# Converting and splitting each unit of weights in one operation, with three tiles in place of four, in a two-layer encoder

## The chip, the cores and the metric

The kernel runs on one core of one Trainium2 chip. Its time is the device time of one execution in microseconds (us). Before the change the median of three runs is 2588.59 us (2588.29 to 2591.06). A separate execution was profiled; all views of the profile are of that one.

The engines are called PE (matrix products; PEld is its loading of stationary operands), DVE (vector), ACT (scalar), POOL, and SP, whose queue issues the transfers between HBM and on-chip memory (SBUF).

## The reference, cut to what matters

Two layers over 256 tokens of width 2048. All weights are float32 and each is read once.

```python
for l in range(DEPTH):                                  # 2
    mod = c_act @ ada_w[l] + ada_b[l]                   # adaLN: six vectors of 2048
    sh_a, sc_a, gt_a, sh_m, sc_m, gt_m = split(mod, 6)
    h = rmsnorm(x, norm_mix[l]) * (1.0 + sc_a) + sh_a
    qa, ka, va, qb, kb, vb, ga, gb = split_cols(h @ w_in[l])
    ya = window_attention(qa, ka, va, sink_a[l]) @ w_proj_a[l]      # mask |i - j| <= 128
    yb = neighbourhood_attention(qb, kb, vb, rel_bias_b[l]) @ w_proj_b[l]
    x = x + gt_a * ((sigmoid(ga) * ya + sigmoid(gb) * yb) @ w_out[l])
    h = rmsnorm(x, norm_ffn[l]) * (1.0 + sc_m) + sh_m
    u = depthwise_conv(h @ w_up[l], conv_w[l], conv_b[l])
    g, v = split(u, 2)
    x = x + gt_m * ((silu(g) * v) @ w_down[l])
```

## The kernel before

**Products in high and low parts.** PE multiplies operands rounded to a shorter float32 form. To keep float32 accuracy, each operand is split into a high part (the rounded value) and a low part (the rest), and a product is the sum of high x high, high x low and low x high. An ACT copy makes the high part of the weights (line 348), a DVE subtraction the low part (line 349).

**Units of weights.** The host lays out all weight matrices as one sequence of blocks of 128 x 128 in the order of use (`block_stream`, line 100). Sixteen blocks are a unit: 1 MiB, one transfer into a raw tile of 128 x 2048 (line 337). There are 464 units, 232 a layer. `unit_steps` (line 331) takes a raw tile out of four, issues the transfer, and then makes the high and the low part of one half of the unit and of the other, each half in its own `hl` tile of 128 x 2 x 1024, of which there are also four (two units). The raw tile comes free when the second subtraction is done, an `hl` tile when PE has used its eight blocks. `next_block` (line 419) hands out blocks; when a unit is used up it takes the next one, in program order just before that unit's matmuls (in the first 52 units of layer 0 one unit earlier).

**What uses a block.** `feature_block` (line 387) holds the weights still and moves the activations; with `Wide` activations (the FFN) a block is two matmuls, lines 391 and 392, of 512 and 256 columns, so a unit is 32 matmuls; otherwise it is three, lines 395 to 397. `tokens` (line 454, the q, k and v columns) moves the weights instead, lines 464 to 466.

**adaLN.** `ada` (line 229) reads the 12288 x 2048 matrix of a layer as 96 tiles of 1 MiB, and one DVE operation for each (line 248) multiplies it by the activated `c` and sums it up. Except for three tiles at the start these use the same four raw tiles as the weights. `plan` (line 794) sets when they are issued: at the end of a unit, along a table of corners by unit number. In layer 0, between units 108 and 231 that is 63 products, so nearly every second unit. In that stretch (and in layer 1 before unit 76 and from unit 108 on) a product is "patient": its transfer is issued at the end of a unit, and its DVE operation is put in program order behind the splits of the next unit (`use_landed`, line 426) and pinned there.

**Order on the queues.** A framework schedules the program: it gives out tiles as they come free, in the order of the program by priority, and fixes the order of each engine's instructions. SP's queue works in order, so a transfer that waits for a tile holds up those behind it.

**Attention.** Eight heads of mixer A, then eight of mixer B, run as steps between the units. Each head has a score tile `p` out of two. In line 730 DVE adds a mask (A) or a bias (B) to the scores. The mask is one tile that is loaded once (`small`, line 870); the bias of a head is brought by its own transfer into `p` (line 964), one step ahead of its use. In layer 1 all heads, in place of PE, use DVE and POOL to turn the probabilities (`turned_blocks`, line 750).

**Layout.** Several tiles have a few extra columns, and their contents begin 16, 48 or 64 columns in (`OFF`, `ROW`, `led`, `chunks_of`, `paired`); `skip` allocates two small unused tiles.

Of the kernel before, what the change touches and what calls it, by code (L numbers as in the profile page):

```python
# [9 lines left out]
F32 = mybir.dt.float32  # L10
# [126 lines left out]
OFF, ROW = 48, 64  # L137
SPARE = {"y2": ROW}
# [7 lines left out]
def encoder(ctx: ExitStack, tc: tile.TileContext, a: dict, out: bass.AP):  # L146
    nc = tc.nc
    pool = lambda name, bufs, **kw: ctx.enter_context(tc.tile_pool(name=name, bufs=bufs, **kw))
    skips = []

    def skip(n, p=None):

        skips.append((p or pool(f"skip{len(skips)}", 1)).tile([P, n // 4], F32, name=f"skip{len(skips)}"))
        nc.vector.memset(skips[-1][:], 0.0)

    const = pool("const", 1)
    lay = pool("lay", 2)
    rawp = pool("raw", 4)
    hlp = pool("hl", 4)
# [30 lines left out]
    skip(96, const)  # L190
    skip(224)
# [5 lines left out]
    def chunks_of(p, tag, room, name, n=None, apart=True):  # L197

        n = n or room
        t = p.tile([P, room * 2 * S + SPARE.get(tag, 0)], F32R, name=name, tag=tag)
        at = [2 * S * k + (ROW - OFF if apart and k == n - 1 and (k < room - 1 or tag in SPARE) else 0) for k in range(n)]
        return [t[:, i : i + 2 * S].rearrange("p (a s) -> p a s", a=2) for i in at]

    def led(name, apart=None):

        t = hp.tile([P, KC * 2 * S + OFF + ROW], F32R, name=name, tag="h")
        at = [0] + [OFF + 2 * S * k for k in range(1, KC)]
        if apart:  # L210
            at[apart] += ROW - OFF
            at[apart + 1 :] = [i + ROW for i in at[apart + 1 :]]
        return [t[:, i : i + 2 * S].rearrange("p (a s) -> p a s", a=2) for i in at]

    def paired(dt, name, at=ROW - OFF):

        t = ev.tile([P, 2 * S + ROW], dt, name=name, tag="u", bufs=2)
        return t[:, at : at + 2 * S].rearrange("p (a s) -> p a s", a=2)
# [112 lines left out]
    def unit_steps(l, u, by_halves=False):  # L331

        raw = rawp.tile([P, UB * P], F32, name=f"w{l}_{u}", tag="raw")
        if not by_halves:
            nc.sync.dma_start(raw[:], a["ws"][l, u])
        halves = []
        streamed = any(m == "w_in" and mo < GATE_A // P for m, _, mo in STREAMS[l][u * UB : (u + 1) * UB])
        at = OFF if streamed else 0  # L340
        for j in range(2):
            n = UB * P // 2
            hl = hlp.tile([P, 2 * n + ROW], F32R, name=f"hl{l}_{u}_{j}", tag="hl")
            hl = hl[:, at : at + 2 * n].rearrange("p (a n) -> p a n", a=2)
            r = raw[:, j * n : (j + 1) * n]
            if by_halves:
                nc.sync.dma_start(r, a["ws"][l, u][:, j * n : (j + 1) * n])
            nc.scalar.copy(hl[:, 0], r)  # L348
            nc.vector.tensor_tensor(out=hl[:, 1], in0=r, in1=hl[:, 0].bitcast(F32), op=ALU.subtract)  # L349
            halves.append(hl)  # L350
            if j == 0:
                yield halves
# [34 lines left out]
    def feature_block(ps, hl, j, act, first, last):  # L387

        hi, lo = hl[:, 0, j * P : (j + 1) * P], hl[:, 1, j * P : (j + 1) * P]
# [9 lines left out]
    class Stream:  # L399
# [54 lines left out]
        def tokens(self, h, kcs):  # L454

            pss = [mm.tile([P, 512], F32, name=f"ps{self.l}_{self.u}_t{t}", tag="mm") for t in range(2)]
            for kc in kcs:
# [3 lines left out]
                hi, lo = (turns(hl[:, i, j * P : (j + 4) * P]) for i in range(2))  # L461
# [44 lines left out]
    class Squares:  # L506
# [6 lines left out]
        def add(self, mo):  # L513
            sq = self.acc if mo == 0 else ev.tile([P, S], F32, name="sq", tag="r", bufs=2)
# [67 lines left out]
    class Bare:  # L582
# [4 lines left out]
        def __init__(self, l, w, sums):  # L587
# [7 lines left out]
            for tag in homes + ["qn"]:  # L595
# [3 lines left out]
                for i in range(k):  # L599

                    off = 2 * self.half * i + (0 if self.chunks else ROW - OFF)
                    c = t[:, off : off + 2 * self.half].rearrange("p (a s) -> p a s", a=2)
                    self.chunks.append((turns(c[:, 0, : S + 2]), turns(c[:, 1, :S])))
# [21 lines left out]
        def roots(self):  # L625
            self.rbs = spread(self.rs)
            self.h = led(f"h{self.l}_{self.w}")
# [668 lines left out]
```

## Time and profile before

| | us |
|---|---|
| median of three runs | 2588.59 |
| the profiled execution | 2583.21 |
| its span, first to last instruction | 2581.4 |
| PE busy | 2549.9 |
| DVE busy | 2209.4 |
| ACT busy | 1450.7 |
| all splits, line 349, 928 of 1225 ns | 1131.3 |
| all high parts, line 348, 928 of 1046 ns | 965.2 |
| all adaLN products, line 248, 189 of 2350 ns and three more | 443.9 |

The granted clock is 0.999 of full speed. In a list of groups a row is: line, engine, operation, out<-in, shapes, number, then busy time, mean ns of one, idle time ahead and what ended it. In a timeline a row is: start, length, engine and line, operation. Where neighbours overlap, the chain of waits gives the time that each holds it, less than its length. "DMA share" in the table by stretches is the mean busy share of the 16 DMA engines.

### The profile page before, as it was taken

How to read it: one execution, taken by the hardware profiler on the slowest of the kernel's cores; microseconds unless marked ns; L12 is line 12 of the kernel's file. 1: busy time of each engine (PE TensorE's matmuls, PEld its weight loads, DVE VectorE, ACT ScalarE, POOL GpSimd, SP SyncE). 2: the span in 40 equal slices, each digit the busy share in tenths (PEclk: the TensorE clock that was granted, in tenths of full speed). 3: DMA queues.
4: the chain of work that ended last, by engine and by line, in shares of the span. 5: the costliest groups of instructions: out<-in, count | busy, mean ns of one | idle time of the engine just before them, and what ended most of it. 6: DMA issues, size and time to landing. Idle time of an engine off the chain costs nothing.

```text
span 2581.4 us, 43559 instructions
## 1 busy us (share of the span) xinstructions
PE 2549.9 (99%) x17324; PEld 2377.2 (92%) x17324; DVE 2209.4 (86%) x3227; ACT 1450.7 (56%) x2432; POOL 246.0 (10%) x345
## 2 busy tenths in 40 slices
PE   8999999999999999999999999999999999999999
PEld 7999899999999998998898889999999999999998
DVE  8998998998998989889997778878889987766775
ACT  5445765456663655455565666555576546644663
POOL 0001100000000000000002668630000000000000
PEclk9999999999999999999999999999999999999999
DMA  9998789986788777877776657667848775555554
GB/s 369 353 349 306 264 296 353 342 317 224 262 319 304 291 291 293 326 291 282 283 257 246 260 212 256 250 260 291 298 166 293 291 295 198 205 201 198 204 202 147
DMA packets 102158, 699.99 MB, mean 271 GB/s; under 512 B 12865, under 2 KB 15169, under 8 KB 18113
## 3 DMA queue, kind: packets, MB, share of 16 engines
q1 hardware_dynamic: 101954, 697.20, 73.3%
q8 instruction: 136, 2.23, 0.3%
q14 instruction: 68, 0.56, 0.1%
HBM read 695.06 MB, written 2.10 MB: 270 GB/s over the span
## 4 chain that ended last, share of the span: by engine, by line
PE 67%; DVE 19%; ACT 5%; issue 4%; POOL 3%; DMA 3%; ACTq 0%; DVEq 0%; POOLq 0%; SPq 0%
PE ps L391 24%; PE ps L392 12%; DVE hl L349 8%; PE ps L397 7%; PE ps L395 7%; PE ps L396 7%; DVE aw L248 3%; ACT hl L348 3%; PE ps_t L466 2%; PE ps_t L465 2%; PE ps_t L464 2%; DVE u L1135 1%; DMA w<-in_ws 1%; POOL packA L320 1%; POOL p L320 1%
## 5 line engine op out<-in xcount | busy, mean ns | idle before, releaser
L349 DVE TENSOR_TENSOR hl<-w,hl 128x1024 fp32r<-128x1024 f32 x928 | 1131.3, 1225 | 237.9 <-ACT hl L348 235.4
L348 ACT CAST hl<-w 128x1024 fp32r<-128x1024 f32 x928 | 965.2, 1046 | 583.9 <-PE ps L392 231.6
L391 PE MATMUL ps<-h,hl 128*128 128x512 f32 x2432 | 797.4, 382 | 0.0
L392 PE MATMUL ps<-h,hl 128*128 128x256 f32 x2432 | 664.0, 273 | 2.8 <-DVE hl L349 2.8
L391 PEld LDWEIGHTS ps<-h,hl 128*128 128x128 f32 x2432 | 459.7, 189 | 63.7
L392 PEld LDWEIGHTS ps<-h,hl 128*128 128x128 f32 x2432 | 466.9, 192 | 5.7 <-DVE hl L349 5.6
L248 DVE CUSTOM_DVE_ANT_0 aw<-aw,cact,ab 128x2048 f32<-128x2048 f32 x189 | 443.9, 2350 | 11.4 <-DMA aw<-in_aw 11.1
L395 PE MATMUL ps<-h,hl 128*128 128x256 f32 x896 | 247.3, 276 | 1.9 <-DVE ri L745 0.8
L396 PE MATMUL ps<-h,hl 128*128 128x256 f32 x896 | 246.4, 275 | 0.0
L397 PE MATMUL ps<-h,hl 128*128 128x256 f32 x896 | 245.8, 275 | 0.0
L464 PE MATMUL ps_t<-hl,h 128*128 128x512 f32 x576 | 217.6, 382 | 3.5 <-ACT h L571 2.3
L465 PE MATMUL ps_t<-hl,h 128*128 128x512 f32 x576 | 219.2, 381 | 1.4 <-DVE hl L349 1.2
L466 PE MATMUL ps_t<-hl,h 128*128 128x512 f32 x576 | 218.5, 380 | 0.0
L395 PEld LDWEIGHTS ps<-h,hl 128*128 128x128 f32 x896 | 171.9, 192 | 3.1 <-ACT hl L348 1.0
L396 PEld LDWEIGHTS ps<-h,hl 128*128 128x128 f32 x896 | 172.0, 192 | 0.4 <-DVE h L572 0.2
L391 PE MATMUL ps<-act_o,hl 128*128 128x512 f32 x512 | 171.1, 382 | 0.6 <-ACT hl L348 0.6
L397 PEld LDWEIGHTS ps<-h,hl 128*128 128x128 f32 x896 | 171.6, 192 | 0.0
L1135 DVE SCALAR_TENSOR_TENSOR u<-both,cw,u 128x255 f32<-128x255 f32 x304 | 146.0, 480 | 2.9
L392 PE MATMUL ps<-act_o,hl 128*128 128x256 f32 x512 | 139.9, 273 | 1.6 <-DVE hl L349 1.6
L397 PE MATMUL ps<-merged,hl 128*128 128x256 f32 x512 | 140.9, 275 | 0.6 <-DVE hl L349 0.6
L396 PE MATMUL ps<-merged,hl 128*128 128x256 f32 x512 | 140.7, 275 | 0.0
L395 PE MATMUL ps<-merged,hl 128*128 128x256 f32 x512 | 140.5, 275 | 0.0
(242 smaller groups left out, 4852.7 us busy)
## 6 DMA issues: line engine op xcount, KB each, us to landing
w<-in_ws SPq DMA_DIRECT2D x463, 1024.0 KB, 4.8
aw<-in_aw SPq DMA_DIRECT2D x189, 1024.0 KB, 5.2
p<-in_bias SPq DMA_DIRECT2D x16, 256.0 KB, 4.6
x<-in_xT SPq DMA_DIRECT2D x4, 512.0 KB, 5.4
aw_o<-in_aw SPq DMA_DIRECT2D x2, 1024.0 KB, 12.6
out<-x SPq DMA_DIRECT2D x16, 128.0 KB, 2.3
w<-in_ws SPq DMA_DIRECT2D x2, 512.0 KB, 11.8
aw_b<-in_aw SPq DMA_DIRECT2D x1, 1024.0 KB, 18.0
```

What stands on the lines that cost most here:

```text
L248: product = nc.vector.tensor_tensor_reduce(out=raw[:], in0=raw[:], in1=cact[:], scale=1.0, scalar=ab[:, i : i + 1], op0=ALU.mult, op1=ALU. ...
L348: nc.scalar.copy(hl[:, 0], r)
L349: nc.vector.tensor_tensor(out=hl[:, 1], in0=r, in1=hl[:, 0].bitcast(F32), op=ALU.subtract)
L391: nc.tensor.matmul(ps[:], hi, act.both, start=first, stop=False)
L392: nc.tensor.matmul(ps[:, :S], lo, act.high, start=False, stop=last)
L395: nc.tensor.matmul(out, hi, act[0], start=first, stop=False)
L396: nc.tensor.matmul(ps[:, :S], hi, act[1], start=False, stop=False)
L397: nc.tensor.matmul(out, lo, act[0], start=False, stop=last)
L464: nc.tensor.matmul(ps[:], xh, hi, start=kc == kcs[0], stop=False)
L465: nc.tensor.matmul(ps[:], xh, lo, start=False, stop=False)
L466: nc.tensor.matmul(ps[:], xl, hi, start=False, stop=kc == kcs[-1])
L1135: nc.vector.scalar_tensor_tensor(out=u[:, to], in0=ps[:, of], scalar=w[:, j : j + 1], in1=u[:, to], op0=ALU.mult, op1=ALU.add)
```

## The change

It replaces the two half-unit operations by one for the whole unit on ACT and one on DVE (the first unit of all, whose transfer comes in two halves, is still done by halves). A split unit is now one tile of 128 x 2 x 2048, and there are three of them; of raw tiles there are three too. The constants of the adaLN plan stay.

Room is found elsewhere: all extra columns and shifted offsets go, and the `skip` tiles with them; the mask of mixer A is no longer kept but brought from HBM into `p` for every head, directly ahead of that head's scores; the convolution weights `cw` are loaded after the attention into a tile shared with it; the squares `sq` use the tiles of tag `z` instead of two of their own.

```diff
-    rawp = pool("raw", 4)
-    hlp = pool("hl", 4)
+    rawp = pool("raw", 3)
+    hlp = pool("hl", 3)
...
-    skip(96, const)
-    skip(224)
...
-    def led(name, apart=None):
-
-        t = hp.tile([P, KC * 2 * S + OFF + ROW], F32R, name=name, tag="h")
-        at = [0] + [OFF + 2 * S * k for k in range(1, KC)]
...
+    def chunks_of(p, tag, room, name, n):
+
+        t = p.tile([P, room, 2, S], F32R, name=name, tag=tag)
+        return [t[:, i] for i in range(n)]
+
+    def halved(name):
+
+        return chunks_of(hp, "h", KC, name, KC)
...
         raw = rawp.tile([P, UB * P], F32, name=f"w{l}_{u}", tag="raw")
+        hl = hlp.tile([P, 2, UB * P], F32R, name=f"hl{l}_{u}", tag="hl")
+        n = UB * P // 2
+        pieces = [slice(0, n), slice(n, 2 * n)]
+        halves = [(hl[:, 0, r], hl[:, 1, r]) for r in pieces]
         if not by_halves:
+            pieces = [slice(0, 2 * n)]
             nc.sync.dma_start(raw[:], a["ws"][l, u])
-        halves = []
-        streamed = any(m == "w_in" and mo < GATE_A // P for m, _, mo in STREAMS[l][u * UB : (u + 1) * UB])
-        at = OFF if streamed else 0
-        for j in range(2):
-            n = UB * P // 2
-            hl = hlp.tile([P, 2 * n + ROW], F32R, name=f"hl{l}_{u}_{j}", tag="hl")
-            hl = hl[:, at : at + 2 * n].rearrange("p (a n) -> p a n", a=2)
-            r = raw[:, j * n : (j + 1) * n]
+        for r in pieces:
             if by_halves:
-                nc.sync.dma_start(r, a["ws"][l, u][:, j * n : (j + 1) * n])
-            nc.scalar.copy(hl[:, 0], r)
-            nc.vector.tensor_tensor(out=hl[:, 1], in0=r, in1=hl[:, 0].bitcast(F32), op=ALU.subtract)
-            halves.append(hl)
-            if j == 0:
-                yield halves
+                nc.sync.dma_start(raw[:, r], a["ws"][l, u][:, r])
+            nc.scalar.copy(hl[:, 0, r], raw[:, r])
+            nc.vector.tensor_tensor(out=hl[:, 1, r], in0=raw[:, r], in1=hl[:, 0, r].bitcast(F32), op=ALU.subtract)
+            yield halves
...
-            sq = self.acc if mo == 0 else ev.tile([P, S], F32, name="sq", tag="r", bufs=2)
+            sq = self.acc if mo == 0 else ev.tile([P, S], F32, name="sq", tag="z")
...
     def small(l):
 
-        if l == 0:
-            tables.append(load(a["maskA"], [P, 2, S], "maskA"))
...
-        cw = load(a["cw"][l], [P, 2 * FC, 4], f"cw{l}", lay, tag="cw", bufs=1)
...
             p = at.tile([P, 2, S], F32, name="p", tag="p")
+            nc.sync.dma_start(p[:], a["maskA"])
...
             yield from attend(
-                q, k, v, p, tables[0], SCALE, sink[:, i : i + 1], lambda: oA[i], rows if i < MOVED[l][0] else None
+                q, k, v, p, p, SCALE, sink[:, i : i + 1], lambda: oA[i], rows if i < MOVED[l][0] else None
             )
...
         bg.finish(job)
-        merged = led(f"merged{l}")
+        cw = load(a["cw"][l], [P, 2 * FC, 4], f"cw{l}", at, tag="qh", bufs=1)
+        merged = halved(f"merged{l}")
```

More of the change, by code (lines that the diff above doesn't have):

```diff
@@ L195, in place, with paired @@
         return sp.tile([P, n, S], dt, name=name, tag=tag)
[L197 to L204, printed above, removed]
-    def led(name, apart=None):
-        t = hp.tile([P, KC * 2 * S + OFF + ROW], F32R, name=name, tag="h")
-        at = [0] + [OFF + 2 * S * k for k in range(1, KC)]
[L210 to L218, printed above, removed]
+    def chunks_of(p, tag, room, name, n):
[3 more added lines that the diff above has]
+        return chunks_of(hp, "h", KC, name, KC)
+    def paired(dt, name):
+        return ev.tile([P, 2, S], dt, name=name, tag="u", bufs=2)[:]
     mods, amods, nrms, done = {}, {}, {}, {0: 0, 1: 0}
@@ L460, in tokens @@
                 j -= 3
-                hi, lo = (turns(hl[:, i, j * P : (j + 4) * P]) for i in range(2))
+                hi, lo = (turns(half[:, j * P : (j + 4) * P]) for half in hl)
                 for t, ps in enumerate(pss):
@@ L888, in small @@
             rots.append(rot)
-        return gains, sink, cw, rots
+        return gains, sink, rots
     for l in range(L):
@@ L895, in encoder @@
         if l == 0:
[L896 removed]
+            h = halved("h0_0")
             first.append(ada_and_h(first_h(h)))
```

23 lines of the change are left out of this document (7 added, 16 removed).

## The prediction

> **What bounds the kernel now.** I read first the page's head, then a table by stretches (busy time and number of instructions of PE, PEld, DVE, ACT, POOL; then clock, DMA share, GB/s), then who waits for whom.
>
> ```profile
> span 2581.4 us, 43559 instructions
> PE 2549.9 (99%) x17324; PEld 2377.2 (92%) x17324; DVE 2209.4 (86%) x3227; ACT 1450.7 (56%) x2432; POOL 246.0 (10%) x345
> ```
> ```profile
> 19.00:130.00 111.00, 105.75 (x627) 93.45 (x628) 101.06 (x119) 57.25 (x82) 0.00 (x0) 1.00 0.97 364
> 387.00:478.00 91.00, 91.00 (x810) 90.79 (x809) 80.49 (x103) 45.23 (x76) 0.00 (x0) 1.00 0.94 357
> 678.10:1307.10 629.00, 623.15 (x3776) 568.19 (x3775) 573.32 (x810) 338.47 (x508) 0.00 (x0) 1.00 0.80 298
> 1420.00:1613.00 193.00, 188.37 (x1109) 171.18 (x1108) 150.03 (x228) 125.34 (x271) 140.81 (x203) 0.99 0.65 243
> 2130.00:2517.00 387.00, 387.00 (x2365) 355.87 (x2364) 288.17 (x407) 218.35 (x317) 0.00 (x0) 1.00 0.57 201
> ```
> PE is busy nearly everywhere. In the FFN a unit (16 blocks) is 32 matmuls, so 2130 to 2517, with nothing in PE's way, gives 387 x 32 / 2365 = 5.24 us a unit, 10.47 for two. The stretch 678 to 1307 holds 3776 / 32 = 118 units: 5.33 each, 11 us over PE's rate. So there is little to win, and what matters is whether three raw tiles still feed PE at 10.47 us per two units.
>
> ```profile
> SPq L337 <- DVE hl L349: 1052.4, 248, 12.3
> SPq L245 <- DVE hl L349: 323.1, 97, 8.9
> SPq L337 <- DVE mod L248: 296.6, 121, 5.9
> PE ps L392 <- DVE hl L349: 5.6, 15, 1.2
> ```
> These are waits (us in total, times, longest). The queue of transfers waits all the time, for DVE to finish with a raw tile. PE itself waits for DVE only 5.6 us. So raw tiles are always all taken, and a transfer starts when one comes free.
>
> Two cuts of the timeline, SP and DVE, in the up-projection of layer 0 (start, length, engine):
>
> ```profile
> 940.89 0.33 SPq L245 DMA_DIRECT2D aw<-in_aw  x1
> 945.87 2.99 SPq L337 DMA_DIRECT2D w<-in_ws  x2
> 951.94 0.33 SPq L245 DMA_DIRECT2D aw<-in_aw  x1
> 956.92 3.00 SPq L337 DMA_DIRECT2D w<-in_ws  x2
> ```
> ```profile
> 944.61 1.23 DVE L349 TENSOR_TENSOR hl<-w,hl 128x1024 fp32r<-128x1024 f32 x1 [1.16 <-ACT hl L348]
> 945.75 0.48 DVE L1135 SCALAR_TENSOR_TENSOR u<-both,cw,u 128x255 f32<-128x255 f32 x1
> 946.15 2.35 DVE L248 CUSTOM_DVE_ANT_0 aw<-aw,cact,ab 128x2048 f32<-128x2048 f32 x1
> ...
> 955.66 1.23 DVE L349 TENSOR_TENSOR hl<-w,hl 128x1024 fp32r<-128x1024 f32 x1 [1.16 <-ACT hl L348]
> ...
> 957.20 2.35 DVE L248 CUSTOM_DVE_ANT_0 aw<-aw,cact,ab 128x2048 f32<-128x2048 f32 x1
> ```
> One period is 11.05 us (946.15 to 957.20): two units and one adaLN product. The first of the two w transfers starts at 945.87, 0.03 after the split that ends at 945.84; the second (0.33 long, ending at 948.86) starts at 948.53, 0.03 after the product that ends at 948.50. The order on SP is aw, w, w; the order in which DVE frees tiles is unit d, its product, unit c. With four tiles transfer k takes the tile freed by the (k-4)th before it: the w of the next d starts when d is freed, a whole period ahead.
>
> **The change, part by part.**
>
> *The merged operations.*
>
> ```profile
> L349 DVE TENSOR_TENSOR hl<-w,hl 128x1024 fp32r<-128x1024 f32 x928 | 1131.3, 1225 | 237.9 <-ACT hl L348 235.4
> L348 ACT CAST hl<-w 128x1024 fp32r<-128x1024 f32 x928 | 965.2, 1046 | 583.9 <-PE ps L392 231.6
> L478 DVE TENSOR_TENSOR act_o<-u,act_o 128x256 fp32r<-128x256 f32 x32 | 13.4, 419 | 1.6 <-ACT act_o L477 1.6
> L477 ACT CAST act_o<-u 128x256 fp32r<-128x256 f32 x32 | 13.0, 406 | 32.0 <-DVE u L1174 32.0
> ```
> ```profile
> 40.66 2.28 DVE hl L349 x2
> 42.93 2.26 DVE aw L248
> ```
> By the slope from 256 to 1024 columns, a cast of 2048 is 1046 + 1024 x (1046 - 406) / 768 = 1899 ns, a split 1225 + 1024 x (1225 - 419) / 768 = 2300 ns. What DVE gains is less than two fixed parts: in the chain two halves hold it 2.28 us, and the one-piece product of 2048 holds it 2.26. So 0.02 to 0.08 us a unit (2.28 less 2.20 to 2.26; the 2.20 is 2.30 less the 0.1 by which neighbours overlap, 1.225 against 1.14), times 464 units: 9 to 37 us of DVE's time, of which PE's waits could return 5.6. I take -3 us.
>
> [...]
>
> From landing to the first usable weights it was 1.05 + 1.23 = 2.28 us, and is now 1.90 + 2.30 = 4.20; to the release of the raw tile about 3.4 (1.05 + 1.14 + 1.23, half of the chain's 2.28 for the first split) and now 4.20. Where PE follows a landing at once (the start) that shifts it once: +2 us.
>
> *Three raw tiles.* This is the main term. With three, transfer k takes the tile freed by the (k-3)rd: aw gets d's tile, and the w of the next d gets the product's. That w is then bound in a loop: d is freed; product, 948.50 - 945.84 = 2.66 us; issue 0.03; transfer; cast 1.90; split 2.30; and the next d is freed.
>
> ```profile
> w<-in_ws SPq DMA_DIRECT2D x463, 1024.0 KB, 4.8
> aw<-in_aw SPq DMA_DIRECT2D x189, 1024.0 KB, 5.2
> ```
> 2.66 + 0.03 + 4.8 + 1.90 + 2.30 = 11.7 us; I take 11.8 with hand-offs. With four tiles the product was not in it (0.03 + 4.8 + 3.4 = 8.2, below 10.47), so it bound nothing. Now it is over PE's 10.47, and a steady loop can't be hidden by buffers, only its first 5.2 us by the one more unit that three whole split tiles hold. How often:
>
> ```profile
> 678.00:1308.00 630.00, 142.06 (x121) 1.00 0.80 298
> ```
> This is L248 alone in that stretch, two instructions a product: 60 products for 118 units, 58 with two units and 2 with one (9.1 us by the same sum without the product). 58 x 11.8 + 2 x 9.1 = 703, against 629: +74, less 5 for the deeper buffer: **+69**. Ends: 11.3 (cast and product overlapping other work) gives +39, 12.7 (transfer at 5.2, the cast behind one 0.4 us operation) +120. Elsewhere products come every third unit or are used on landing, and three tiles in turn need some 9 us per three units.
>
> Two stretches are at the transfers' own limit (0.97 and 0.94 of the DMA engines above):
>
> ```profile
> 61.22 0.33 SPq L337 DMA_DIRECT2D w<-in_ws  x1
> ...
> 95.86 0.33 SPq L337 DMA_DIRECT2D w<-in_ws  x1
> ```
> ```profile
> 400.99 0.33 SPq L337 DMA_DIRECT2D w<-in_ws  x1
> ...
> 445.25 0.33 SPq L245 DMA_DIRECT2D aw<-in_aw  x1
> ```
> That is 12 and 15 steps: 2.89 and 2.95 us a tile, each tile held four of these, 11.6 us. Unhindered a w needs 4.8 + 4.2 = 9.0 and an aw 5.2 + 2.35 = 7.6, a mean of 8.3: over three tiles 2.77, no loss. If holding didn't shrink it would be 11.6 / 3 = 3.9, a third longer, +67 over both. With two in flight at 2.9 each I take 5.8 a transfer and 0.5 of queueing, 9.6 / 3 = 3.2, 10% of 202 us, less the 5 of the buffer: **+15**.
>
> *The mask by a transfer for every head.* It goes on SP ahead of later weights, waits for a `p` tile, and L730 waits for it in DVE's order with the splits behind it.
>
> ```profile
> 1509.15 0.68 DVE L484 TENSOR_TENSOR pT<-p,pT 128x512 fp32r<-128x512 f32 x1
> ...
> 1510.09 0.48 DVE L730 CUSTOM_DVE_ANT_0 p<-sc,maskA,sink 128x256 f32<-128x256 f32 x1
> ```
> ```profile
> p<-in_bias SPq DMA_DIRECT2D x16, 256.0 KB, 4.6
> ```
> In layer 1 a head's `p` is freed by this L484 and the head after next wants its mask 0.3 us later: about 4.3 us of DVE standing still, for some six heads, 26 us. DVE idles 193 - 150 = 43 us in that stretch and PE has units in hand: from 0 to +26, I take +5, the nearer end to its idle time.
>
> *Free.* `cw` is loaded later but far ahead of its use; `sq` shares `z`, idle in those stages. Plain offsets in the tiles:
>
> ```profile
> L392 PE MATMUL ps<-h,hl 128*128 128x256 f32 x2432 | 664.0, 273 | 2.8 <-DVE hl L349 2.8
> L392 PE MATMUL ps<-act_o,hl 128*128 128x256 f32 x512 | 139.9, 273 | 1.6 <-DVE hl L349 1.6
> ```
> `h` lies at shifted offsets of its tile, `act` at plain ones, and both run at 273 ns: 0. A nanosecond either way on 17324 matmuls would be 17 us, the bound both ways.
>
> Sum: -3 + 2 + 69 + 15 + 5 = +88 on the profiled execution's 2583.2 (span 2581.4): 2671. That execution is 5.4 below the median of 2588.6, so **2676 us**.
>
> **The rivals.** *Faster: the product leaves the loop.* If the schedule puts the w transfer ahead of aw, or frees the product's tile first, the loop is 9.1 < 10.47 (that is where it decides) and only the gains count: DVE's saving and a third unit in hand return the 11 us over PE's rate, and some of the start: 2574. For: SP's order need not stay. Against: aw comes ahead of w in program order and the product is pinned behind its unit's split. 0.13.
>
> *No change.* Loop just under PE's rate, gains against masks: 2589. 0.08.
>
> *Slower by masks and start alone:* 15 + 2 + 5 to 26 - 3, up to +40 without the loop: 2608 (2594 to 2630). 0.17. [...]
>
> **How the numbers follow.** Forecast 0.62, its own range 2630 to 2740. A change of 0.2%, 5 us, is about what a measurement can tell. Slower 0.17 + 0.62 = 0.79, same 0.08, faster 0.13. The range 2590 to 2740 leaves out the faster case, half of the unchanged one and a few hundredths above.
>
> **What would show it.** In the stretch of 118 units: 703 us in place of 629, PE idle with waits for L349 of 1.3 us per product, SP waiting for L248 before the first of two w, transfers of aw starting at the end of a split. L349 at 2.30, L348 at 1.90. L730 waiting for DMA in layer 1. I am wrong if that stretch holds 629 or less, or if 2130 to 2517, where no product comes, changes its 5.24 us a unit.

## The result, and the profile after

The changed kernel took 2778.37 us (median of 6 runs, 2774.41 to 2794.14) against 2589.39 us for the kernel before (6 runs, 2587.71 to 2591.06): the ratio is 1.0741, 95% interval 1.0726 to 1.0757. I had forecast 2676, so 87 us more; it became 189. The sign and the main place were right, the size was less than half. A few executions of the kernels below, and of the one before beside them, were far longer than the rest (4731 to 9445 us); the ratios leave them out, and without them no median would move by 1 us.

The head of the page after, with the chain of waits by engine:

```profile
span 2772.6 us, 42391 instructions
PE 2612.7 (94%) x17324; PEld 2399.8 (87%) x17324; DVE 2176.6 (79%) x2762; ACT 1384.0 (50%) x1969; POOL 244.0 (9%) x345
PE 30%; DVE 28%; DMA 20%; ACT 12%; issue 6%; POOL 4%; ACTq 0%; SPq 0%; DVEq 0%; POOLq 0%
```

The span is 191.2 us longer than the 2581.4 of before, and PE is now idle for 160 us (2772.6 less 2612.7) where it was idle for 31.5. The same stretches as in the prediction, cut where the same units begin (columns: length, then busy time and instructions of PE, PEld, DVE, ACT, POOL, then clock, DMA share, GB/s):

```profile
18.90:139.20 120.30, 108.91 (x627) 95.54 (x628) 99.99 (x101) 56.07 (x63) 0.00 (x0) 0.97 0.86 328
406.40:498.80 92.40, 91.50 (x810) 90.91 (x809) 75.21 (x86) 42.72 (x59) 0.00 (x0) 1.00 0.87 337
709.40:1442.40 733.00, 656.84 (x3772) 576.41 (x3770) 573.98 (x690) 327.62 (x390) 0.00 (x0) 0.98 0.67 254
1559.70:1772.40 212.70, 194.43 (x1109) 173.87 (x1108) 145.25 (x192) 115.01 (x229) 133.31 (x196) 0.97 0.62 228
2321.10:2708.10 387.00, 387.00 (x2365) 355.94 (x2364) 274.48 (x334) 204.99 (x244) 0.00 (x0) 1.00 0.56 200
```

The 118 units with a product in every second one took 733 us, not 629, and not the 703 of the forecast. The last stretch, without products, is 387.00 as before: PE's rate of 5.24 us a unit did not change, so the plain layout costs nothing there. Laid against the same stretches of before, these five lost 9.3, 1.4, 104.0, 19.7 and 0 us, 134.4 of the 191.2; the other 57 us went between them: 10.2 after the first, 10.5 after the second, 4.4 after the third, 31.7 after the fourth. Who waits for whom, first on SP's queue, then on ACT and PE (us in total, times, longest; L321 issues the weights, L224 the adaLN tiles, L227 is the product, L325 the cast, L326 the split):

```profile
SPq L321 <- DVE hl L326: 854.3, 225, 12.4
SPq L321 <- DVE mod L227: 238.4, 98, 5.5
SPq L224 <- DVE hl L326: 237.8, 66, 6.1
```
```profile
ACT hl L325 <- DMA w<-in_ws: 476.8, 193, 9.9
PEld ps L367 <- DVE hl L326: 111.8, 103, 2.1
PE ps L367 <- DVE hl L326: 77.5, 66, 1.8
```

PE's matmuls on the low half (L367) waited 77.5 us for the split; the like row of before was 5.6. And the casts wait for DMA, 476.8 us: the chain now runs from a transfer to the cast, the split and PE. One period in the up-projection of layer 0, SP and DVE:

```profile
1003.67 0.33 SPq L224 DMA_DIRECT2D aw<-in_aw  x1
1006.61 3.04 SPq L321 DMA_DIRECT2D w<-in_ws  x2
1015.65 0.33 SPq L224 DMA_DIRECT2D aw<-in_aw  x1
```
```profile
1001.35 2.29 DVE L326 TENSOR_TENSOR hl<-w,hl 128x2048 fp32r<-128x2048 f32 x1 [1.23 <-ACT hl L325]
...
1004.23 2.34 DVE L227 CUSTOM_DVE_ANT_0 aw<-aw,cact,ab 128x2048 f32<-128x2048 f32 x1
...
1006.97 2.28 DVE L326 TENSOR_TENSOR hl<-w,hl 128x2048 fp32r<-128x2048 f32 x1
...
1013.33 2.29 DVE L326 TENSOR_TENSOR hl<-w,hl 128x2048 fp32r<-128x2048 f32 x1 [1.18 <-ACT hl L325]
...
1016.21 2.34 DVE L227 CUSTOM_DVE_ANT_0 aw<-aw,cact,ab 128x2048 f32<-128x2048 f32 x1
...
1018.87 2.28 DVE L326 TENSOR_TENSOR hl<-w,hl 128x2048 fp32r<-128x2048 f32 x1
```

Here the loop is the one that was forecast: d's split ends at 1003.64, the aw transfer takes its tile at 1003.67, the product ends at 1006.57, the w of the next d takes the product's tile at 1006.61, and its split ends at 1015.62: 11.98 us a period. The signs that the prediction named are there: whole splits of 2.29 us, SP waiting for the product ahead of the first w, PE waiting for the split. The same rows give a way to count that the prediction lacked: the time for which each tile is held. This aw is held from 1003.67 to the end of its product at 1018.55, 14.9 us; d from 1006.61 to 1015.62, 9.0; c from 1009.32 (the second of the two issues) to 1021.15, 11.8. Together 35.7, over three tiles 11.9 us. At the 4.6 us that the next aw (issued at 1015.65) took to land, some 8 of the 14.9 pass after the landing, waiting for the pinned place behind the next unit's split. As an account this always closes: where every tile is taken again at once, the times held add up to three periods, whatever sets the period. It becomes a forecast only with the times for which the tiles would be held if nothing in the ring waited.

### The profile page after: what moved, and what is told of

Its sections match the earlier page's. It is cut to its first block, busy times and chain, and to the rows that moved or that the text cites. A ratio compares the mean times of both kernels' runs of the same rounds, so it can differ in the third digit from the quotient of the medians.

```text
span 2772.6 us, 42391 instructions
## 1 busy us (share of the span) xinstructions
PE 2612.7 (94%) x17324; PEld 2399.8 (87%) x17324; DVE 2176.6 (79%) x2762; ACT 1384.0 (50%) x1969; POOL 244.0 (9%) x345
## 4 chain that ended last, share of the span: by engine, by line
PE 30%; DVE 28%; DMA 20%; ACT 12%; issue 6%; POOL 4%; ACTq 0%; SPq 0%; DVEq 0%; POOLq 0%
DMA w<-in_ws 18%; DVE hl L326 14%; PE ps L366 13%; ACT hl L325 9%; DVE aw L227 7%; PE ps L367 7%; PE ps L372 3%; PE ps L370 3%; PE ps L371 3%; POOL packA L299 1%; POOL p L299 1%; DMA aw<-in_aw 1%; DVE u L1106 1%; PE ps_t L440 1%; POOL qrs L510 1%
## 5 line engine op out<-in xcount | busy, mean ns | idle before, releaser
L326 DVE TENSOR_TENSOR hl<-w,hl 128x2048 fp32r<-128x2048 f32 (+1 forms) x465 | 1063.7, 2288 | 376.8 <-ACT hl L325 375.9
L325 ACT CAST hl<-w 128x2048 fp32r<-128x2048 f32 (+1 forms) x465 | 884.3, 1902 | 656.2 <-DMA w<-in_ws 476.8
L366 PE MATMUL ps<-h,hl 128*128 128x512 f32 x2432 | 808.7, 385 | 4.9 <-ACT hl L325 4.9
L367 PE MATMUL ps<-h,hl 128*128 128x256 f32 x2432 | 673.6, 277 | 46.0 <-DVE hl L326 44.6
L367 PEld LDWEIGHTS ps<-h,hl 128*128 128x128 f32 x2432 | 470.2, 193 | 65.6 <-DVE hl L326 65.6
L227 DVE CUSTOM_DVE_ANT_0 aw<-aw,cact,ab 128x2048 f32<-128x2048 f32 x189 | 443.5, 2348 | 9.0 <-DMA aw<-in_aw 8.8
L440 PE MATMUL ps_t<-hl,h 128*128 128x512 f32 x576 | 223.1, 388 | 17.2 <-DVE hl L326 17.0
L439 PE MATMUL ps_t<-hl,h 128*128 128x512 f32 x576 | 218.7, 386 | 5.5 <-ACT hl L325 3.5
L441 PE MATMUL ps_t<-hl,h 128*128 128x512 f32 x576 | 220.5, 384 | 0.0
L1128 ACT COPY both<-ps 128x256 f32<-128x256 f32 x152 | 56.3, 371 | 282.4 <-PE ps L367 282.3
L1079 DVE SCALAR_TENSOR_TENSOR x<-ps,mod,x 128x256 f32<-128x256 f32 x224 | 105.1, 480 | 70.0 <-PE ps L367 67.0
L367 PE MATMUL ps<-act_o,hl 128*128 128x256 f32 x512 | 141.5, 278 | 11.2 <-DVE hl L326 11.2
L370 PE MATMUL ps<-merged,hl 128*128 128x256 f32 x512 | 143.0, 280 | 6.2 <-DVE m L472 6.2
```

The costliest lines, as they stand in the source:

```text
L227: product = nc.vector.tensor_tensor_reduce(out=raw[:], in0=raw[:], in1=cact[:], scale=1.0, scalar=ab[:, i : i + 1], op0=ALU.mult, op1=ALU. ...
L325: nc.scalar.copy(hl[:, 0, r], raw[:, r])
L326: nc.vector.tensor_tensor(out=hl[:, 1, r], in0=raw[:, r], in1=hl[:, 0, r].bitcast(F32), op=ALU.subtract)
L366: nc.tensor.matmul(ps[:], hi, act.both, start=first, stop=False)
L367: nc.tensor.matmul(ps[:, :S], lo, act.high, start=False, stop=last)
L370: nc.tensor.matmul(out, hi, act[0], start=first, stop=False)
```

## The experiments

The table holds what each kernel loses against before in five groups of units, from the times at which PE begins them (us, profiled executions; the last units lose under 2 in any, and a group and its total can differ by where PE begins the first unit, 2 us at most). Layer 0 is units 0 to 231, its attention about 44 to 68; the units 231 to 300 hold the attention of layer 1, and 300 to 390 include a second stretch of pinned products. Raw is the number of raw tiles, ops the operations for a conversion.

| kernel | raw | ops | 0-58 | 58-112 | 112-231 | 231-300 | 300-390 | all |
|---|---|---|---|---|---|---|---|---|
| changed | 3 | 1 | 19.5 | 11.9 | 105.4 | 26.6 | 27.9 | 191.1 |
| e1 before, three raw | 3 | 2 | 11.5 | 11.2 | 58.7 | 4.0 | 28.7 | 114.3 |
| e2 four raw, two split | 4 | 1 | 14.4 | 20.3 | -3.0 | 19.2 | 24.3 | 76.9 |
| e3 product first | 3 | 1 | 21.0 | 6.5 | 117.7 | 16.0 | 32.0 | 193.1 |
| e4 before, masks | 4 | 2 | -0.3 | 5.9 | 0.8 | 1.3 | 0.2 | 8.2 |
| e5 unpinned | 3 | 1 | 22.0 | 13.2 | -4.1 | 25.5 | 2.2 | 59.7 |
| e6 two operations | 3 | 2 | 10.8 | 3.8 | 62.9 | 14.8 | 12.4 | 104.6 |
| e7 four raw, five halves | 4 | 2 | 1.9 | -1.3 | -4.2 | 3.9 | -1.5 | -0.3 |
| e9 two ops, unpinned | 3 | 2 | 11.8 | 6.0 | 15.3 | 14.6 | 8.7 | 56.3 |
| e10 e2 with two ops | 4 | 2 | 4.5 | 8.0 | 9.6 | 5.1 | 11.4 | 38.7 |
| e11 before, unpinned | 4 | 2 | -0.3 | 4.0 | 20.9 | -1.3 | 4.4 | 27.9 |
| e12 e7 unpinned | 4 | 2 | 4.8 | 0.9 | 1.7 | 4.3 | 2.8 | 16.6 |
| e14 own tile | 3 | 1 | 21.2 | 15.9 | -12.3 | 26.4 | 21.6 | 73.1 |

**Tiles or operations (e1, e2, e6).** The kernel before with three raw tiles:

```diff
-    rawp = pool("raw", 4)
+    rawp = pool("raw", 3)
```


> The kernel before, with three raw tiles instead of four and nothing else changed (split in halves, four half split tiles, resident mask, shifted layout). Theory (the adaLN product sits in the loop of a weight transfer as soon as three tiles serve three transfers per two units): the loop is 0.03 + 2.66 + 4.8 + 3.4 = 10.9 us where nothing else stands on DVE, a little over PE's 10.47, and longer where other work stands between split and product; so the 118 units from 108 on take 640 to 700 us instead of 658, and the whole 2610 to 2700. Rival 1 (the longer latency of whole operations, 4.2 us against 2.3, is what costs, not the count of tiles): 2589 within 0.3%. Rival 2 (all of the loss is the tile count, whatever the operations): 2740 or more.

2692.68 us, ratio 1.0388 (1.0362 to 1.0414): within the theory's range for the whole, though not for the stretch: the units 108 to 231 took 717 us, and it allowed 640 to 700. Three tiles alone cost 103 us (114.3 in the profiled execution, 58.7 of them in the units from 112 to 231), though nothing else was changed. Then the changed kernel with four raw tiles, and two whole split tiles to pay for the fourth:

```diff
-    rawp = pool("raw", 3)
-    hlp = pool("hl", 3)
+    rawp = pool("raw", 4)
+    hlp = pool("hl", 2)
```


> The changed kernel with four raw tiles and two split tiles of a whole unit (in place of three and three); whole operations, a mask transfer per head and the plain layout stay. Theory: with four tiles the product is out of the loop, the loop is 0.03 + 4.8 + 4.2 = 9.0 per two units, the stretch from unit 108 to 231 returns from 767 us to 655 to 670, and the whole to 2590 to 2640 with what the mask costs left. Rival 1 (whole operations cost by their latency): the loss stays or grows, since only two whole units are ahead of PE: 2740 or more. Rival 2 (the plain layout slows PE): PE's 5.24 us a unit where no product comes would be longer.

2661.82 us, 1.0267 (1.0243 to 1.0292). The stretch came back whole, as the theory had it:

```profile
712.70:1339.50 626.80, 622.40 (x3775) 567.98 (x3774) 565.00 (x688) 324.18 (x390) 0.00 (x0) 1.00 0.80 297
```

626.8 us for the 118 units, with whole operations. But the total is 22 us over the theory's range: 14 us are lost at the start, 20 before unit 112, 43 from 231 to 390, far more than the masks cost (e4, below). And the changed kernel with its tiles, but two operations for a conversion:

```diff
         if not by_halves:
-            pieces = [slice(0, 2 * n)]
             nc.sync.dma_start(raw[:], a["ws"][l, u])
```


> The changed kernel, with three raw and three whole split tiles, but each unit converted and split by two operations again, in halves of its tile. Theory: a raw tile is held 0.8 us less (3.4 against 4.2 us from landing to release), so two units and a product take (10.1 + 10.1 + 14) / 3 = 11.4 us in place of 12.3, and PE can start on a first half earlier: the stretch from unit 108 to 231 falls by some 50 us to 710 to 725, and the whole to 2690 to 2730. Rival (the merging is neutral or a gain and the tiles are all): 2770 or more, a few us of DVE's time on top.

2692.06 us, 1.0397 (1.0376 to 1.0418), as expected. So the merging is no small thing: with three raw tiles it costs 86 us of the 189, and what is left, 102, is what three tiles alone cost in e1. In the profiles 42.5 of the 86 are in the stretch, where a raw tile held longer, 0.8 us by my estimate (4.20 less 3.4 from landing to release), lengthens the loop each time, 15.5 in the units 300 to 390, 12 in layer 1's attention (26.6 against 14.8), 9 at the start and 8 in the units 58 to 112. With four tiles it is 14 at that attention (19.2 in e2, 5.1 in e10). The prediction had priced the longer operations at 2 us.

**What was left in e2 (e10).** The kernel of e2 with two operations, in halves of its two whole tiles; the edit is that of e6.

> The changed kernel with four raw tiles and two whole split tiles (2662 us), but each unit converted and split in two operations, in halves of those whole tiles. It tells what the 72 us are that were left there. If it is the length of the operations: 2590 to 2605. If it is that a whole split tile comes free only when PE is through the whole unit: 2650 to 2665, the two operations changing nothing. Theory: both, the operations the larger part: 2600 to 2635.

2622.12 us, 1.0123 (1.0109 to 1.0137), in the middle of the theory's range: 40 of the 72 us were the long operations; what is left, 31 us, may be the masks (4 us in e4) and two split tiles that come free only as wholes; this run does not part them. In the units 112 to 231 it is the other way round: there the whole operations of e2 are 13 us ahead of these halves (-3.0 against 9.6). So in these runs merging cost where tiles were short, and gained where the ring was not the limit.

**The order of the product (e3).**

```diff
             if self.at == UB:
+                use_landed()
                 if self.ahead:
...
                 self.u, self.at = self.u + 1, 0
-                use_landed()
```


> The changed kernel with one line moved: in the stretches where the adaLN product is pinned, it is pinned ahead of the conversion of the next unit and not behind it; three raw tiles and everything else stay. Theory: the product's tile is then free before the unit's split ends, the weight transfer takes the split's own tile and its loop is 0.03 + 4.8 + 4.2 = 9.0 us in place of 11.9; the stretch from unit 108 to 231 falls from 767 us to 655 to 700, the whole to 2660 to 2710. Rival 1 (latency of the whole operations) and rival 2 (three tiles are too few for the bandwidth whatever the order): no gain, 2765 to 2790.

2780.73 us, 1.0732 (1.0703 to 1.0762): no gain, as the rivals had it; the theory, as I had put it then, failed. The SP and DVE rows show why.

```profile
1031.87 3.51 SPq L321 DMA_DIRECT2D w<-in_ws  x2
1040.88 0.33 SPq L224 DMA_DIRECT2D aw<-in_aw  x1
1044.30 3.51 SPq L321 DMA_DIRECT2D w<-in_ws  x2
```
```profile
1032.67 2.35 DVE L227 CUSTOM_DVE_ANT_0 aw<-aw,cact,ab 128x2048 f32<-128x2048 f32 x1
...
1038.55 2.29 DVE L326 TENSOR_TENSOR hl<-w,hl 128x2048 fp32r<-128x2048 f32 x1 [1.06 <-ACT hl L325]
...
1041.97 2.29 DVE L326 TENSOR_TENSOR hl<-w,hl 128x2048 fp32r<-128x2048 f32 x1 [0.46 <-ACT hl L325]
...
1045.10 2.34 DVE L227 CUSTOM_DVE_ANT_0 aw<-aw,cact,ab 128x2048 f32<-128x2048 f32 x1
```

The product now follows c's split instead of d's, and the second w (1035.05) takes its tile; the period is 12.43 us (1032.67 to 1045.10). The aw issued at 1040.88 lands at 1045.67 by the trace (in the changed kernel an aw took 4.6 us or more to land), so it isn't the one that is used at 1045.10: it is used a period on, and held still longer. So the product still stands in the loop of a weight transfer, now that of c. It seems not to matter which transfer follows the product, but that a landed aw holds one of three tiles; e14 tests that. From here on the theory was in tiles: period = time held, over the number of tiles.

**No pins (e5, e9, e11, e12).**

```diff
-        patient[0] = u >= HASTE.stop or l > 0 and u < HASTE.start
+        patient[0] = False
```


> The changed kernel with no adaLN product pinned: each may be placed as soon as its transfer lands. Theory, now in terms of tiles: the period of two units is the time that the three tiles of the period are held, divided by three. In the changed kernel that is (10.9 + 10.9 + 15.0) / 3 = 12.3 us, and 8 of the 15.0 of an aw tile are spent landed and waiting for its pinned place. Unpinned, it is held 8 to 9, and (9.0 + 9.0 + 8.5) / 3 = 8.8, below PE's 10.47: the stretch from unit 108 to 231 falls from 767 us to 655 to 690, the whole to 2650 to 2690. Rival (the order of pinning moves nothing, as with the product put first; the transfers or DVE are the limit): 2765 to 2790.

2642.55 us, 1.0199 (1.0178 to 1.022): 136 us less, a little better than the theory's range. One period:

```profile
1000.46 0.33 SPq L224 DMA_DIRECT2D aw<-in_aw  x1
```
```profile
1005.29 2.35 DVE L227 CUSTOM_DVE_ANT_0 aw<-aw,cact,ab 128x2048 f32<-128x2048 f32 x1 [0.22 <-DMA aw<-in_aw]
```

The aw of 1000.46 is used as it lands and free at 1007.64, held 7.2 us in place of 14.9; the 118 units took 625.0, PE's rate but for a few us. In the units 300 to 390, too, 26 of the 28 us are gone. With two operations for a conversion as well:

> The changed kernel with both edits: no product pinned, and each unit converted and split in two operations; three raw and three whole split tiles stay. Alone the first gave 2643 and the second 2692, from 2778. Theory (the units from 108 to 231 suffer from the held aw tile, made longer by the merged operations; the start and the attention of layer 1 suffer from three tiles and from merged operations, about half each): the stretch from 108 to 231 is as long as before, within 5 us, the start keeps 10 of its 20 us and the attention 12 of its 23, the whole is 2610 to 2625. Rival (start and attention are lost to three tiles alone): 2635 to 2645. Rival (to the merged operations alone): 2590 to 2600.

2637.44 us, 1.0182 (1.0164 to 1.02): a miss by 12 us. It lies in the range of the rival "three tiles alone", but not for the rival's reason: start (11.8) and layer 1's attention (14.6 in its group) kept about what the theory expected, and the units 112 to 231 lost 15.3 of their own. The next run loses 20.9 there, also without pins and with two operations; e5, without pins but with whole operations, loses nothing. So it is not the absence of pins alone, and the cause stays open. The kernel before, unpinned:

> The kernel before with no adaLN product pinned; four raw tiles. Theory: with four tiles the period may hold 4 x 10.47 = 41.9 us of tile time and two units and a pinned product there hold about 12.1 + 12.1 + 17.6, which includes waiting for nothing that hurts; shortening the last gains nothing: 2580 to 2595, the same within 0.2%. Rival (the pinned products cost in any kernel, and the gain of 136 us in the changed kernel shows it): 2570 or less.

2618.83 us, 1.0111 (1.009 to 1.0132): neither theory nor rival. With four tiles and operations in halves the pins are worth 27 us (against 2591.45 for the kernel before beside it); 21 of them are in the same units. So pins are no loss in themselves: they cost 136 us only where an adaLN tile held by them is missing elsewhere. And the layout and masks of the change, four raw tiles and halves, without pins (kernel e7, below, with the same edit):

> The changed kernel's layout and masks with units in halves, four raw and five half split tiles (2584 us with pinned products), and no product pinned. Theory: tiles are not short here, so the place of the products matters little: 2577 to 2592, the same as with pinned ones within 0.3%. If the whole of it is faster than the kernel before by more than 0.2%, the fifth half tile has paid for the masks and more.

2600.14 us, 1.0034 (1.0019 to 1.0048): 8 us above the theory's range, and 16 us more than with pins.

**The same tiles, divided by role (e13, e14, e15).** Pins, whole operations and three raw tiles stay, but from unit 108 to 231 of layer 0 adaLN has one tile and the weights have two:

```diff
+    def raw_tile(name, product=False):
+        turn[0] += not apart[0]
+        third = product if apart[0] else turn[0] % 3 == 0
+        return rawp.tile([P, UB * P], F32, name=name, tag="one" if third else "raw", bufs=1 if third else 2)
...
-            nc.sync.dma_start(raw[:], a["aw"][l, n])
+            (nc.gpsimd if apart[0] else nc.sync).dma_start(raw[:], a["aw"][l, n])
```


> The changed kernel, with the same three raw tiles, whole operations and pinned products; but from unit 108 to 231 the adaLN transfers have one of the three for themselves and are issued on POOL's queue, which is idle there, so that a held aw tile takes none from the weights and its wait stops no weight transfer; the weights have the other two. Theory (what costs is that a pinned product holds a tile that the next weights need): a w tile is held some 9.3 to 10.5 us, two of them serve two units in that time, the stretch from 108 to 231 falls from 767 us to 655 to 690. The start may move a little, since there the three are taken in turn. Whole: 2670 to 2705. Rival (the pins or the length of the whole operations disturb DVE's order by themselves): the stretch stays over 730, the whole over 2740.

> The same tiles as in the run beside it (two for weights, one for adaLN, from unit 108 to 231), but the adaLN transfers stay on SP's queue ahead of the weights. Theory: the next adaLN transfer waits on SP until the product has freed its tile, and the weight transfers behind it wait with it; the product is in the weights' loop again, by the queue and not by the tile: the stretch at 740 us or more, the whole at 2755 or more. Rival (only the sharing of tiles costs): as in the run beside it, under 2710.

In e14 the last edit is left out. e13 took 2658.13 us (1.0256, 1.0236 to 1.0276), e14 2661.45 us (1.0268, 1.0251 to 1.0284): e13 goes the theory's way and 12 us past its range, and for e14 the rival holds. The queue costs nothing that can be told from noise; in these units the sharing of tiles costs everything. The 118 units of e14:

```profile
715.40:1333.30 617.90, 617.90 (x3775) 568.21 (x3774) 567.79 (x688) 326.53 (x389) 0.00 (x0) 1.00 0.82 304
```

PE is busy for all of 617.90 us: this is PE's own rate, 5.24 us a unit, 11 us better than the kernel before, with one raw tile fewer, the pins, and whole operations. The same division in layer 1, too, from unit 108 to 142 there:

```diff
-        apart[0] = l == 0 and HASTE.stop <= u < NU - 1
+        apart[0] = HASTE.stop <= u < (NU - 1 if l == 0 else ADA_PLAN_1[-1][0])
```


> The changed kernel with its three raw tiles divided by role, two for weights and one for adaLN, from unit 108 on in both layers, as long as products come (units 108 to 231 of layer 0, units 108 to 142 of layer 1); all on SP's queue. In layer 0 alone this gave 2661. Theory (the 16 us lost at units 360 to 390 are the same held tile): 12 to 18 us less than 2661: 2643 to 2650. Rival (that stretch, with products twice as far apart, loses by something else): 2655 to 2665.

2642.83 us, 1.0205 (1.0192 to 1.0218): 18 us less, what the theory had, though in the profile the units 344 to 390 give back only 9 of e14's 15.6 us; the second stretch has the same cause in the main. (The profiled execution of e15 was the slowest of those counted, 2649.83 us.)

**The masks (e4, e8).**

```diff
             p = at.tile([P, 2, S], F32, name="p", tag="p")
+            nc.sync.dma_start(p[:], a["maskA"])
...
-                q, k, v, p, tables[0], SCALE, sink[:, i : i + 1], lambda: oA[i], rows if i < MOVED[l][0] else None
+                q, k, v, p, p, SCALE, sink[:, i : i + 1], lambda: oA[i], rows if i < MOVED[l][0] else None
```


> The kernel before, with the mask of part A brought by a transfer into the p tile of each head, as in the changed kernel; everything else of before stays (the resident mask is still loaded, unused, so that no address moves). Theory: the transfers wait for p tiles at the head of SP's queue and the first operation on a head waits for them on DVE; in layer 1 some 4.3 us for each of a few heads, 10 to 30 us in all: 2600 to 2620. Rival (with four raw tiles the units in hand cover it): 2589 within 0.2%; the attention's share of the loss then needs the three tiles.

2593.52 us, 1.0011 (0.9998 to 1.0023): the rival, and no difference clear of noise. In the profile next to nothing is lost in either attention; 5 us are in the units 84 to 90 of layer 0, long after it. In the changed kernel, with the mask's transfer moved ahead of the yield in a head:

```diff
             k = kvs[0]
-            yield
             p = at.tile([P, 2, S], F32, name="p", tag="p")
             nc.sync.dma_start(p[:], a["maskA"])
+            yield
```


> The changed kernel with the mask's transfer issued one step of a head earlier, as that of the bias is. Theory: of the 22 us that the attention of layer 1 (units 252 to 300) lost, part is DVE waiting for masks; it falls by 5 to 20, the whole to 2755 to 2773. Rival (that loss is the three tiles and the pinned products alone; with four tiles the masks cost 4 us in all): within 5 us of 2778.

2784.93 us, 1.0751 (1.0735 to 1.0767): no gain, the rival again, though 6.6 us over the changed kernel where it allowed 5. A row of the waits of the changed kernel would have said it at once; this is all that DVE waits for masks:

```profile
DVE p L704 <- DMA p<-in_maskA: 3.0, 2, 2.0
```

**Everything else of the change, and versions that might win (e7, e16, e17).** Units in halves again, each half in a tile of its own:

```diff
-    rawp = pool("raw", 3)
-    hlp = pool("hl", 3)
+    rawp = pool("raw", 4)
+    hlp = pool("hl", 5)
...
+            hl = hlp.tile([P, 2, n], F32R, name=f"hl{l}_{u}_{r.start}", tag="hl")
```


> The changed kernel with units in halves again, four raw tiles and five half split tiles (what the room holds); masks by transfer per head and plain layout stay. Theory: neither tiles nor long operations are missing, so only the masks' few us remain: 2580 to 2600, and the start (units 0 to 58) within 3 us of before. Rival (the plain layout, the shared sq tile or the late cw cost something by themselves): 2610 or more.

2584.39 us, 0.9984 (0.9974 to 0.9994): plain layout, masks per head, late `cw` and shared `sq` together cost nothing once tiles are enough. The 4 us gained in the units 112 to 231 may be the fifth half tile's; no run isolates it. It is the fastest version found, by 0.16%. Roles on top, for the kernel before and for e7 (three tiles for weights, one for adaLN):

> The kernel before with its four raw tiles divided by role in the same units, three for weights and one for adaLN; nothing else changed. Theory: the units from 108 to 231 took 658 us where PE's own rate gives 123 x 5.24 = 644; with the held aw tile out of the weights' way they come within 4 us of that: 2575 to 2584. Rival (with four tiles the product takes nothing from the weights): 2587 to 2593.

> The changed kernel's layout and masks with units in halves, four raw and five half split tiles (2584 us), the raw tiles divided by role as in the run beside it. Theory: there 7 of the 13 us over PE's rate are left in the units from 108 to 231, so the gain is smaller: 2575 to 2582. Rival: no change, 2582 to 2588.

2596.99 us (1.0034, 1.0022 to 1.0046) and 2589.14 us (1.0, 0.9991 to 1.0009): both miss. The units 112 to 231 gain 2.3 and 8.5 us on the kernel before, but outside them these versions hand out tiles in fixed turn and not as they come free, which may be why the units up to 112 lose 15.7 and 9.1.

## Why the prediction was wrong, and where it was right

**Where the missing 103 us are.** The forecast was 88 us more, and the span grew by 191. By the stretches that the prediction had cut, the 118 units lost 104 in place of 69, the two stretches at the transfers' limit (a DMA share of 0.97 and 0.94 before) 11 in place of 15, layer 1's attention 20 in place of 5. The other 57 us lie where the prediction put nothing. So two steps failed: the smaller is the period of the loop (35 us), the larger is what was put at nothing elsewhere, by the sentence on three tiles in turn and by the merging's +2 (57 us).

**Three raw tiles, the main term: right in kind, too small.** The step that failed here is "I take 11.8 with hand-offs" for a period, used for 58 periods to make 703 us. The loop is the one forecast, but in regular rows of the up-projection its period is 11.95 to 12.0, since two DVE operations of 0.42 us stand between the split and the product, which ends 2.93 us after the split and not 2.66. Over the 118 units 733 us / 59 is 12.4: other periods are longer. One shows how; in ACT's rows, a copy that waits for PE stands ahead of a cast:

```profile
950.17 0.37 ACT L1128 COPY both<-ps 128x256 f32<-128x256 f32 x1 [7.34 <-PE ps L367]
...
951.54 1.89 ACT L325 CAST hl<-w 128x2048 fp32r<-128x2048 f32 x1
```

The w of this cast was issued at 944.49 and had landed at 949.19 by the trace. PE was late, since it had waited and then ran at half its rate (below), so the cast began 2.35 us after the landing, and the period from 942.12 took 14.2 us. How much of the step from 12.0 to 12.4 this makes was not measured. The upper end that I had given, +120, held the measured +104.

**"Elsewhere products come every third unit or are used on landing, and three tiles in turn need some 9 us per three units": failed.** It put at nothing what became 57 us. For the units 300 to 390, which lost 27.9 us, it counted no waiting for the pin: e5 takes the pins away and 2.2 are left. The units 58 to 112 lost 11.9, and 13.2 without pins; e1, with three tiles alone, loses 11.2 there. How it arises in these units was not traced.

**The merged operations: failed.** "Where PE follows a landing at once (the start) that shifts it once: +2 us." Undoing the merging alone gives back 86 us (e6). Of these 42.5 are in the 118 units, whose loop was summed with the whole operations' lengths; the other 44 stand against that +2. Where a tile's turn was the limit, those 0.8 us a turn (an estimate, 4.20 less 3.4) would be paid in each; and near attention, it seems, PE waits for a whole split where half would do. A row of layer 1 shows such a wait:

```profile
1585.84 0.48 PE L440 MATMUL ps_t<-hl,h 128*128 128x512 f32 x1 [4.17 <-DVE hl L326]
```

How the 12 us in layer 1's attention arise operation by operation was not tried.

**DVE's saving: 0.02 to 0.08 us a unit was right where operations are packed, and it bought nothing that shows.** In the last stretch, alike in both kernels, DVE is busy 274.48 us in place of 288.17: with 73.9 units (2365 / 32), 0.185 us each. There the halves do not run back to back, and two of them cost more than one whole operation by about the 0.16 us by which 2 x 1.225 exceeds 2.29. In the 118 units it is 573.98 against 573.32 in the changed kernel, but 565.0 in e2 and 567.8 in e14, where the same operations keep up with PE: 0.05 to 0.07 us a unit less. In the last stretch PE was the limit, so DVE's saving shortened nothing.

**The start: the sum near, the place by luck.** +15 was forecast for the two stretches at the transfers' limit (those with a DMA share of 0.97 and 0.94 before), which lost 9.3 and 1.4. The units 0 to 58 lost 19.5 because 10 more went between these stretches, where no term stood. Nor is it three tiles alone: two operations take it to 10.8 (e6), four tiles to 14.4 (e2), both, with the split tiles in halves, to 1.9 (e7).

**The masks: small, as taken.** +5 was forecast; e4 gives 4, not clear of noise, with four tiles. In the changed kernel L704 waited for a mask twice, both times in layer 1's attention, 3.0 us in all: not in six heads, and not for 4.3 us each. So DVE's waiting for masks is not the 20 us lost in that attention. What the prediction did not price is SP: there the mask transfers (L916) stood 32 us in all at the head of the queue until a `p` came free, with weights behind them, and 32 in e8 too. With four raw tiles, in e4, they stood as long and little was lost; with three it may be part of the loss, which no run isolates. **Layout, `cw`, `sq` at 0: right** by the last stretch and by e7.

**The rivals.** "The product leaves the loop" did not happen by itself; its price for the 118 units, the 11 us over PE's rate, was right when it was made to happen (618 us in e14). The sum by the five groups: forecast 88 = 69 + 17 + 5 - 3; measured 191.1 = 19.5 + 11.9 + 105.4 + 26.6 + 27.9 less 0.2 of rounding. What stays open: how masks, three tiles and whole split tiles share the 15 us that e6 still loses in the units 231 to 300 (e1, with three raw tiles but no masks, loses 4 there), and why unpinned products cost 21 us in the kernel before, where e5 loses nothing.

## What to carry to other kernels

Count a ring of buffers by time held: the sum, over one period, of the time from a transfer's issue to its tile's release, divided by the number of tiles, must stay under the period of the engine that is to be the limit; take the times without the waits that the ring itself makes, since with these the sum always closes. A tile that waits for a place pinned in an engine's order counts for all of that wait (here 14.9 us, against 7.2 without the pin); give such transfers a tile of their own, or let them go early, before taking tiles from the rest. Count the length of the operations in each turn of such a ring, too. Here merging cost 86 us with three shared tiles, and gained 13 to 19 us in the units 112 to 231 where the ring was not the limit (e2 against e10, e5 against e9).

## What the runs showed of the hardware

In one irregular period of the changed kernel, also in the up-projection, PE lost more than the time it waited:

```profile
936.53 0.27 PE L367 MATMUL ps<-h,hl 128*128 128x256 f32 x1
939.59 0.48 PE L366 MATMUL ps<-h,hl 128*128 128x512 f32 x1 [2.79 <-ACT hl L325]
941.92 0.58 PE L367 MATMUL ps<-h,hl 128*128 128x256 f32 x1 [1.84 <-DVE hl L326]
942.29 0.64 PE L366 MATMUL ps<-h,hl 128*128 128x512 f32 x1
942.72 0.42 PE L367 MATMUL ps<-h,hl 128*128 128x256 f32 x1
942.94 0.64 PE L366 MATMUL ps<-h,hl 128*128 128x512 f32 x1
...
948.01 0.38 PE L366 MATMUL ps<-h,hl 128*128 128x512 f32 x1
948.23 0.27 PE L367 MATMUL ps<-h,hl 128*128 128x256 f32 x1
948.33 0.38 PE L366 MATMUL ps<-h,hl 128*128 128x512 f32 x1
```

After waits of 2.79 and 1.84 us a pair of matmuls takes 0.65 us from start to start (942.29 to 942.94) and from 948.01 on 0.32: half the rate from 941.92 on, for 6.1 us, with a granted clock of 0.50 from 941.90 to 948.00, so 3.0 us lost beside the 4.6 waited. After the single waits of the regular periods (four from 1000 to 1050, 1.0 us at most) PE was not slowed; two rows by stretch, the second with these periods, with a granted clock of 1.00 against 0.97:

```profile
900.00:1000.00 100.00, 90.19 (x515) 79.62 (x514) 78.18 (x99) 48.43 (x63) 0.00 (x0) 0.97 0.68 253
1000.00:1050.00 50.00, 46.04 (x270) 40.32 (x269) 40.73 (x52) 26.52 (x34) 0.00 (x0) 1.00 0.71 265
```

The mean granted clock by core bounds how much it was in all:

```profile
core 0: 2772.6 us, clock 0.986
```

Before it was 0.999. If it is a mean over the span, 0.013 of 2772.6 us is 36 us that PE lost (an estimate, since the view does not say how it weighs idle time). That is at most a fifth of the 191; how much of it lengthened the run is not shown, since PE is not the limit in every slow period. Two waits, of 2.79 and 1.84 us with one matmul between them, stood ahead of the 6.1 us of slow time here; what sets such a time off was not shown.
